# Weights of one attention and one scan layer split early, stored and reloaded; silu formed from tanh

## The chip, the cores and the metric

The kernel runs on one core of a Trainium2 chip. The metric is the device time of one execution in microseconds (us). The engines are TensorE (PE in the profile, with its weight loads as PEld), VectorE (DVE), ScalarE (ACT), GpSimd (POOL) and SyncE (SP), which here only issues DMAs.

## The reference

The reference sends 512 tokens of width 1024 through four layers, all in float32: a state-space mixer with a gated output (glu), an attention over a window of 128 tokens, a second state-space layer ("mamba"), and a full attention with two score maps. After the first and the second stands a feed-forward of width 4096 (`h + square(relu(hm @ w_up)) @ w_down`) and a gate (`h + sigmoid(norm(h) @ w_ple_gate) * (p @ w_ple_proj)`). What the change touches:

```python
k = (rmsnorm(h, kv_norm) @ w_k); v = (rmsnorm(h, kv_norm) @ w_v); q = rmsnorm(h, norm_mix) @ w_q
zxbcdt = rms_norm(x, norm_g) @ w_in                       # 1024 x 6176
z, xbc, dt_raw = zxbcdt[:2048], zxbcdt[2048:6144], zxbcdt[6144:]   # by columns
xbc = silu(causal_depthwise_conv(xbc, conv_w, conv_b))    # 4 taps
y = ssd_chunked_scan(xs * dt, a * dt, bm, cm) + d_skip * xs
u = y * silu(z); u = u * rsqrt(mean(u * u over 256 columns) + 1e-5) * gate_norm_g
```

## The kernel before, in words

Activations lie transposed: one tile holds 128 of the 1024 features by 512 tokens. To keep float32 accuracy on a faster matmul type (fp32r), every operand is split into two parts: `hi`, its rounding to fp32r, and `lo`, the rest. A product takes three matmuls (`three`): hi·hi, hi·lo and lo·hi.

Weights are split on the chip too. The class `Weights` holds the whole program's list of units (one DMA each, usually 1024 KB) and chunks (128 output columns by 1024 inputs, 24 matmuls each). `load_to` (L84) issues a unit's load on SP (L88) into one of three `raw` buffers. `split_to` (L92) multiplies a chunk by its norm gain on POOL where it has one (L100, 44 of the 289 chunks split on ACT: those of `w_k`, `w_v`, `w_q`, `w_kv_2` and `b_w_in_2`), rounds it on ACT (`whi`, L103) and subtracts on `lo_eng` (`wlo`, L104). `lo_eng` is DVE, but POOL during the q and v steps of the first attention and during mamba's input steps (L1139, L1410). `whi` and `wlo` have four buffers each. `take`, called by `gemm` before each chunk's matmuls, asks for the split of two chunks further on.

In the feed-forward (`mlp`, L890) the hidden 4096 columns go in two halves: `gemm` over 16 up chunks, whose `up` does relu and square on ACT, the square again on POOL and the rest on DVE; then 8 steps of two down chunks each, whose `down` adds to `h`. It has 64 chunks, and the kernel runs it twice.

In `mamba` (L1172) 48 chunks of `a_w_in_2` make z (16), B and C (8 each) and x (16). `conv` (L1263) takes a product through four taps and a `Silu` on ACT; `evac_z` takes z through `Silu`. Between these, the generator `ssd` does the scan of the previous group in small steps: per head it loads a row of the decay sums, broadcast to 128 partitions, from DRAM (`dec<-acs`, SP, L1331), forms `Exp` of it on ACT, multiplies on DVE, and PE takes the product (`yd`). `gate` (L1358) multiplies by silu(z), sums squares, and takes a root (`Sqrt`) in `rsqrt`. The ACT functions lie in tables that the compiler loads (`ACT_TABLE_LOAD`) when the function needed is not in the loaded one.

The order of instructions on each engine is not the order of the source: the program is built with `schedule_with_timeline_sim=True`, by which a planner reorders each engine's instructions by the times of its own model. Each engine, and SP's queue, then works in the fixed order it was given. Temporary tiles of 2 KB per partition come from 69 slots (`slot`, `drop`).

Of the kernel before, what the change touches and what calls it, by code (L numbers as in the profile page):

```python
# [11 lines left out]
F32 = mybir.dt.float32  # L12
F32R = mybir.dt.float32r
I32 = mybir.dt.int32
ACTF = mybir.ActivationFunctionType
# [47 lines left out]
class Weights:  # L63


    def __init__(self, nc, raw_pool, hl_pool, ahead_dma, ahead_split):
        self.nc, self.raw_pool, self.hl_pool = nc, raw_pool, hl_pool
        self.units, self.chunks = [], []
        self.loaded, self.split, self.used = 0, 0, 0
        self.ahead_dma, self.ahead_split = ahead_dma, ahead_split  # L70
        self.raw, self.hl = {}, {}
        self.lo_eng = nc.vector

    def add(self, w, k0, kt, c0, cols, cut=128, kg=8, gain=None):


        u = len(self.units)
        self.units.append((w[k0:k0 + 128 * kt, c0:c0 + cols].rearrange("(k p) n -> p k n", p=128), kt, cols))
        gain = None if gain is None else (gain, k0 // 128)
        new = [(u, k, min(kg, kt - k), c, min(cut, cols - c), gain) for c in range(0, cols, cut) for k in range(0, kt, kg)]  # L80
        self.chunks.extend(new)
        return new

    def load_to(self, u):  # L84
        while self.loaded < min(u, len(self.units)):
            ap, kt, cols = self.units[self.loaded]
            t = self.raw_pool.tile([128, kt, cols], F32, tag="raw", name="raw")
            self.nc.sync.dma_start(out=t, in_=ap)  # L88
            self.raw[self.loaded] = t
            self.loaded += 1  # L90

    def split_to(self, n):  # L92
        while self.split < min(n, len(self.chunks)):
            u, k, kn, c, cn, gain = self.chunks[self.split]
            self.load_to(u + self.ahead_dma)
            src = self.raw[u][:, k:k + kn, c:c + cn]
# [25 lines left out]
class Builder:  # L122
# [544 lines left out]
    def plan(self):  # L667
        W, ins = self.W, self.ins
        W.add(ins["w_ple_proj"][0], 0, 2, 0, D, cut=512)
        glu = ins["ssm_w_glu"][0]  # L670
        for m in range(0, 8, 2):
            n = len(W.chunks)
            a = W.add(glu, 0, 8, m * 128, 256)
            b = W.add(glu, 0, 8, D + m * 128, 256)
            W.chunks[n:] = [x for p in zip(a, b) for x in p]
        self.plan_mlp_gate(0)
        W.add(ins["w_k"], 0, 8, 0, 256, gain="kv")
        for m in range(0, 8, 2):
            if m == self.V_AT:
                W.add(ins["w_v"], 0, 8, 0, 256, cut=256, kg=4, gain="kv")  # L680
            W.add(ins["w_q"][0], 0, 8, m * 128, 256, gain="mix1")
        W.add(ins["w_ple_proj"][1], 0, 2, 0, D, cut=512)
        for m in range(0, 8, 2):
            W.add(ins["w_o"][0], 0, 8, m * 128, 256)
        self.plan_mlp_gate(1)
        w = ins["a_w_in_2"][0]
        W.add(w, 0, 8, 6144, 32)
        for g in range(self.Z_FIRST):
            W.add(w, 0, 8, 256 * g, 256)
        for g in range(8):  # L690
            W.add(w, 0, 8, 4096 + 128 * g, 128)
            W.add(w, 0, 8, 5120 + 128 * g, 128)
            W.add(w, 0, 8, 2048 + 256 * g, 256)
            if g in self.Z_AT:
                W.add(w, 0, 8, 256 * (self.Z_FIRST + self.Z_AT.index(g)), 256)
        for g in range(self.Z_FIRST + len(self.Z_AT), 8):
            W.add(w, 0, 8, 256 * g, 256)
        for m in range(8):
            W.add(ins["a_w_out_2"][0], 0, 16, m * 128, 128)
        for m in range(0, 8, 2):  # L700
            W.add(ins["w_kv_2"], 0, 8, m * 128, 256, gain="kv2")
        for c in range(2):
            for k0 in (0, 512):
                W.add(ins["w_kv_2"], k0, 4, D + c * 512, 512, cut=512, kg=2, gain="kv2")
        n, w = len(W.chunks), ins["b_w_in_2"][0]
        tiles = dict(x for m in range(0, 8, 2) for o in (0, 8)
                     for x in zip((o + m, o + m + 1), W.add(w, 0, 8, (o + m) * 128, 256, gain="b2")))
        W.chunks[n:] = [tiles[m] for m in self.QG]
        for k0 in (0, 512):
            W.add(ins["b_w_out_2"][0], k0, 4, 0, 512, cut=512, kg=2)  # L710
        for m in (4, 6):
            W.add(ins["b_w_out_2"][0], 0, 8, m * 128, 256, cut=256, kg=4)
# [9 lines left out]
            W.add(ins["w_ple_gate"][i], 0, 8, m * 128, 256)  # L722


    def gemm(self, n, xs, evac, lag=0, hook=None, hook_at=None):

        kt, pend, hook_at = len(xs), deque(), lag if hook_at is None else hook_at
        for m in range(n):
            ps = self.gbank()
            for k0 in range(0, kt, 8):  # L730
                whi, wlo = self.W.take()
# [158 lines left out]
    def mlp(self, xs, acc, name):  # L890
# [8 lines left out]
            r2.append(t)  # L899

        out, acc2 = [], self.slot(F32, "acc")
        for hf in range(2):
# [12 lines left out]
            def down(m, ps):  # L915
                t = self.slot(F32, "t")
                self.tt(t, ps, r2[0], MUL)
                self.tt(self.h[m], self.h[m], t, ADD)
                self.drop(t)
                if hf == 1:  # L920
                    self.square_in(acc2, self.h[m], m)
                    out.append(self.pair(self.h[m], self.g(name, m)))

            self.gemm(16, xs, up, 0 if hf else 1, None if hf else hook)
            if hf == 1:
                for p in xs:
                    self.drop(*p)
            self.gemm(8, hid, down)
            for p in hid:
                self.drop(*p)  # L930
        self.drop(r2[0])
        return out, acc2

    def side_input(self, i):
# [237 lines left out]
    def mamba(self, xs, acc1, acc2):  # L1172
# [8 lines left out]
        A.copy(out=cw, in_=ps[:, :160])  # L1181
        self.drop(*rows)

        hd = const.tile([128, 2, 32], F32, name="hd")
# [10 lines left out]
        with ExitStack() as cx:  # L1195
# [67 lines left out]
            def conv(t, ps):  # L1263
# [94 lines left out]
            def gate(g):  # L1358
# [9 lines left out]
                r = self.rsqrt(acc, 256.0, self.eps5)  # L1368
# [9 lines left out]
                ten[t] = conv((16 + g, 24 + g, 2 * g, 2 * g + 1)[i], ps)  # L1378

            def evac_z(t, ps):  # L1380
                x = self.slot(F32, "z")
# [265 lines left out]
def block_kernel(ctx: ExitStack, tc: tile.TileContext, ins, out, dbg=None):  # L1647
    nc = tc.nc
    b = Builder(ctx, tc, ins, out, dbg)
    raw = ctx.enter_context(tc.tile_pool(name="wraw", bufs=3))  # L1650
    hl = ctx.enter_context(tc.tile_pool(name="whl", bufs=4))
    b.W = Weights(nc, raw, hl, 2, 2)
    b.plan()
    b.add_slots(36, "f")

# [69 lines left out]
```

## Time and profile before

| | us |
|---|---|
| median of 3 runs (2044.8 to 2045.51) | 2044.87 |
| the profiled execution | 2044.02 |
| its span, first to last instruction | 2042.1 |
| PE busy | 1911.3 |
| DVE busy | 1182.1 |
| ACT busy | 970.2 |
| POOL busy | 582.2 |

The span in stages, by the trace: state-space mixer to 199, glu to 275, first feed-forward to 624, its gate and the first attention to 868, second feed-forward to 1197, its gate to about 1270, mamba to 1752 (of it the input steps and scan to 1664), second attention to the end. [...] A line like "PE a <- ACT b" in a list of waits says that PE stood still before it wrote a, until ACT had written b.

### The profile page before, as it was taken

The numbers are of one execution on the slowest core, as the hardware profiler recorded it, in microseconds if no ns is written. First come the engines' busy times: TensorE is split into PE (matmuls) and PEld (weight loads), VectorE is DVE, ScalarE is ACT, GpSimd is POOL, SyncE is SP. The second block draws the span as 40 slices with busy tenths as digits, with TensorE's granted clock in tenths as the row PEclk, the third lists the DMA queues.
The fourth block names the chain that finished last, engine by engine and source line by source line (L and its number), as shares of the span: only waits on it lengthen the run. The fifth ranks groups of instructions, "written<-read, shape, count | busy, mean of one in ns | idle before, by whom it ended". The sixth has DMA issues, their size and how long they took to land.

```text
span 2042.1 us, 25143 instructions
## 1 busy us (share of the span) xinstructions
PE 1911.3 (94%) x9486; PEld 1576.8 (77%) x9486; DVE 1182.1 (58%) x1912; ACT 970.2 (48%) x1734; POOL 582.2 (29%) x381
## 2 busy tenths in 40 slices
PE   2689999999999899999999999888899999999998
PEld 1678888888887787888888887667677788887888
DVE  7896553333447686543333456865457564727885
ACT  4554333223324377443233335587778843334553
POOL 6410122002116730221022008334444443432000
PEclk9899999999999899999999999999999999999999
DMA  4102333333332332232333321332233223335331
GB/s 118 26 6 87 115 104 90 96 103 96 90 103 93 93 115 65 83 104 83 103 104 91 95 86 51 97 104 75 73 101 124 86 74 117 116 91 138 110 94 42
DMA packets 232251, 185.82 MB, mean 91 GB/s; under 512 B 22803, under 2 KB 213982, under 8 KB 232130
## 3 DMA queue, kind: packets, MB, share of 16 engines
q1 hardware_dynamic: 219072, 179.43, 30.2%
q10 hardware_dynamic: 13058, 4.78, 1.0%
q8 instruction: 75, 1.23, 0.3%
q14 instruction: 46, 0.38, 0.1%
HBM read 166.03 MB, written 2.16 MB: 82 GB/s over the span
## 4 chain that ended last, share of the span: by engine, by line
PE 69%; DVE 13%; ACT 9%; issue 4%; POOL 2%; DMA 2%; SPq 0%; ACTq 0%; DVEq 0%; POOLq 0%
PE pg L192 63%; ACT L189 2%; ACT dec L189 2%; DVE lent L173 2%; PE pm L192 1%; PE sc L192 1%; ACT whi L103 1%; DVE dec L173 1%; DVE wlo L104 1%; DMA dec<-acs 1%; DVE pr L184 1%; ACT ea L189 1%; DVE cy L179 1%; DVE h L173 1%; PE po L192 1%
## 5 line engine op out<-in xcount | busy, mean ns | idle before, releaser
L103 ACT ACTIVATE whi<-raw 128x1024 fp32r<-128x1024 f32 x289 | 304.3, 1055 | 689.4 <-PE pg L192 594.9
L192 PE MATMUL pg<-xh,whi 128*128 128x512 f32 x1424 | 566.2, 398 | 10.4 <-ACT xh L189 5.0
L192 PE MATMUL pg<-xl,whi 128*128 128x512 f32 x1424 | 563.3, 396 | 7.4 <-DVE xl L173 7.4
L192 PE MATMUL pg<-xh,wlo 128*128 128x512 f32 x1424 | 561.2, 394 | 0.0
L104 DVE TENSOR_TENSOR wlo<-raw,whi 128x1024 fp32r<-128x1024 f32 (+1 forms) x229 | 296.5, 1297 | 369.1 <-ACT whi L103 369.0
L192 PEld LDWEIGHTS pg<-xh,whi 128*128 128x128 f32 x1424 | 270.5, 190 | 71.0 <-ACT xh L189 5.9
L192 PEld LDWEIGHTS pg<-xl,whi 128*128 128x128 f32 x1424 | 270.7, 190 | 68.3 <-DVE xl L173 10.0
L192 PEld LDWEIGHTS pg<-xh,wlo 128*128 128x128 f32 x1424 | 270.6, 190 | 56.9 <-issue 1.3
L176 POOL TENSOR_TENSOR b<-a 128x512 f32<-128x512 f32 x64 | 99.0, 1546 | 438.1 <-ACT a L189 418.6
L104 POOL TENSOR_TENSOR wlo<-raw,whi 128x1024 fp32r<-128x1024 f32 x60 | 145.3, 2425 | 211.2 <-ACT whi L103 201.3
L192 PE MATMUL pg<-hh,whi 128*128 128x512 f32 x512 | 199.2, 389 | 0.0
L192 PE MATMUL pg<-hl,whi 128*128 128x512 f32 x512 | 199.2, 389 | 0.0
L192 PE MATMUL pg<-hh,wlo 128*128 128x512 f32 x512 | 199.2, 389 | 0.0
L173 POOL TENSOR_TENSOR acc<-acc,sq 128x512 f32<-128x512 f32 x48 | 75.9, 1588 | 316.3 <-ACT sq L189 278.0
L100 POOL TENSOR_TENSOR raw<-raw,gv 128x1024 f32<-128x1024 f32 x44 | 94.5, 2168 | 138.9 <-DMA raw<-in_b_w_in_dram 81.0
L192 PEld LDWEIGHTS pg<-hh,whi 128*128 128x128 f32 x512 | 96.1, 188 | 20.1
L192 PEld LDWEIGHTS pg<-hh,wlo 128*128 128x128 f32 x512 | 96.1, 188 | 19.9
L192 PEld LDWEIGHTS pg<-hl,whi 128*128 128x128 f32 x512 | 96.1, 188 | 19.8
L189 ACT ACT_TABLE_LOAD x68 | 87.2, 1283 | 23.1 <-DVE cy L179 11.2
L173 DVE TENSOR_TENSOR t<-pg,r 128x512 f32<-128x512 f32 x48 | 32.7, 688 | 109.1 <-PE pg L192 109.0
L179 DVE SCALAR_TENSOR_TENSOR cy<-pg,cw,cy 128x511 f32<-128x511 f32 (+2 forms) x96 | 70.5, 738 | 43.4 <-ACT cy L189 42.8
L173 DVE TENSOR_TENSOR hl<-b,hh 128x512 fp32r<-128x512 f32 x64 | 44.1, 691 | 56.9 <-POOL b L176 56.9
(414 smaller groups left out, 3068.1 us busy)
## 6 DMA issues: line engine op xcount, KB each, us to landing
raw<-in_w_up_dram SPq DMA_DIRECT2D x32, 1024.0 KB
raw<-in_w_down_dram SPq DMA_DIRECT2D x32, 1024.0 KB
raw<-in_a_w_in_dram SPq DMA_DIRECT2D x16, 1024.0 KB
raw<-in_ssm_w_glu_dram SPq DMA_DIRECT2D x8, 1024.0 KB
raw<-in_w_ple_gate_dram SPq DMA_DIRECT2D x8, 1024.0 KB
raw<-in_a_w_in_dram SPq DMA_DIRECT2D x16, 512.0 KB
dec<-acs SPq DMA_DIRECT2D x32, 256.0 KB
raw<-in_a_w_out_dram SPq DMA_DIRECT2D x8, 1024.0 KB
```

Source lines behind the costliest of these rows:

```text
L100: self.nc.gpsimd.tensor_tensor(out=src, in0=src, in1=g, op=MUL)
L103: self.nc.scalar.activation(out=hi, in_=src, func=ACTF.Copy)
L104: self.lo_eng.tensor_tensor(out=lo, in0=src, in1=hi.bitcast(F32), op=SUB)
L173: (eng or self.V).tensor_tensor(out=out, in0=a, in1=b, op=op)
L176: self.G.tensor_tensor(out=out, in0=a, in1=b, op=op)
L179: self.V.scalar_tensor_tensor(out=out, in0=a, scalar=s, in1=b, op0=op0, op1=op1)
L184: eng.tensor_scalar(out=out, in0=a, scalar1=s1, scalar2=None, op0=op0)
L189: self.A.activation(out=out, in_=in_, func=func, **kw)
L192: self.T.matmul(out=out, lhsT=lhsT, rhs=rhs, start=start, stop=stop)
```

## The change

Sixty chunks (12 of the first attention: `w_k`, `w_v`, `w_q`; 48 of mamba's `a_w_in_2`) are marked `early`. They are no longer loaded and split beside their own matmuls. Instead each is cut in two pieces of 128 x 512, and `early_step` handles one piece in each of 60 calls per feed-forward: after each `up`, between the two chunks of a `down` step, and after it. A call stores the piece split in the call before (two DMAs of 256 KB, hi and lo, into a DRAM tile), loads a new piece (256 KB), and splits the piece loaded two calls before: gain on POOL if it has one, hi on ACT, lo on DVE. Each of these instructions is tied (`keep_in_program_order`) behind the one that stands before it in the source on its engine. Where the chunk is used, `split_to` only loads hi and lo from DRAM (512 KB each) into `whi` and `wlo`.

In mamba `Silu(y)` becomes `y' * (1 + Tanh(y'))` with `y' = y/2`: the taps and the bias are halved once, `Tanh` runs on ACT into a slot of its own and a `scalar_tensor_tensor` on DVE forms the product. For z it forms twice the silu; the norm's divisor (256 to 1024) and a halved gain take the factor out. The core of the diff:

```diff
+    def early_step(self, b, more=True):
+        nc, last = self.nc, b.tc.keep_in_program_order
+        if self.under_way and len(self.under_way[0]) == 3:
+            (chunk, h), raw, hi = self.under_way.popleft()
...
+            last(nc.sync.dma_start(out=self.kept[chunk][h, 0], in_=hi.bitcast(F32)))
+            last(nc.sync.dma_start(out=self.kept[chunk][h, 1], in_=raw))
+            b.drop(hi)
+        if more and self.n_early < len(self.early):
...
+            raw = self.early_pool.tile([128, 512], F32, tag="eraw", name="eraw", bufs=4)
+            last(nc.sync.dma_start(out=raw.rearrange("p (k n) -> p k n", k=n),
+                                   in_=self.units[u][0][:, k + h * n:k + h * n + n, c:c + cn]))
+            self.under_way.append(((chunk, h), raw))
...
+        if self.under_way and (len(self.under_way) > 2 or not more):
...
+                last(nc.gpsimd.tensor_tensor(out=x, in0=x, in1=g, op=MUL))
+            hi = b.slot(F32R, "ehi")
+            last(nc.scalar.activation(out=hi, in_=raw, func=ACTF.Copy))
+            last(nc.vector.tensor_tensor(out=raw.bitcast(F32R), in0=raw, in1=hi.bitcast(F32), op=SUB))
+            self.under_way[0] = (piece, raw, hi)
+    def early_end(self, b):
+        while self.under_way:
+            self.early_step(b, False)
...
     def split_to(self, n):
...
+            if self.units[u][3]:
+                hi = self.hl_pool.tile([128, kn, cn], F32R, tag="whi", name="whi")
+                lo = self.hl_pool.tile([128, kn, cn], F32R, tag="wlo", name="wlo")
+                for i, t in enumerate((hi, lo)):
...
+                    self.nc.sync.dma_start(out=t, in_=self.kept[chunk][:, i].rearrange("h p n -> p h n"))
...
@@ def up / def down / gemm(8, hid, down, between=half)
+                self.W.early_step(self)
...
+                if hf == 0 or m < 6:
+                    self.W.early_step(self)
+                elif m == 6:
+                    self.W.early_end(self)
@@ mamba: conv
-                self.act(y, y, ACTF.Silu)
+                u = self.slot(F32, "th")
+                self.act(u, y, ACTF.Tanh)
+                self.stt(y, u, 1.0, y, ADD, MUL)
+                self.drop(u)
@@ mamba: evac_z
-                    self.act(x, x, ACTF.Silu)
+                    self.act(u, x, ACTF.Tanh, scale=0.5)
+                    self.stt(x, u, 1.0, x, ADD, MUL)
...
-                    self.act(x, ps, ACTF.Silu)
+                    self.act(u, ps, ACTF.Tanh, scale=0.5)
+                    self.stt(x, u, 1.0, ps, ADD, MUL)
```

## Rows read from the trace of the kernel before

**Rows 1.** The page, parts 1 and 2: busy time by engine, granted clock.

```profile
PE 1911.3 (94%) x9486; PEld 1576.8 (77%) x9486; DVE 1182.1 (58%) x1912; ACT 970.2 (48%) x1734; POOL 582.2 (29%) x381
...
PEclk9899999999999899999999999999999999999999
```

**Rows 2.** Stretches: length, busy us of PE, PEld, DVE, ACT, POOL, PEclk, DMA share, GB/s.

```profile
275.40:624.30 348.90, 348.90 (x1541) 288.99 (x1540) 137.14 (x140) 115.41 (x147) 61.01 (x41) 1.00 0.33 98
624.30:690.00 65.70, 56.57 (x232) 43.93 (x232) 56.84 (x40) 30.20 (x42) 52.25 (x28) 0.94 0.21 66
690.00:818.00 128.00, 124.26 (x840) 104.36 (x840) 88.94 (x202) 83.72 (x235) 36.77 (x20) 0.99 0.36 99
1197.00:1270.00 73.00, 69.78 (x299) 54.72 (x298) 48.66 (x43) 33.55 (x49) 37.21 (x22) 0.98 0.21 61
1270.00:1317.00 47.00, 39.58 (x164) 31.00 (x163) 41.31 (x55) 27.38 (x34) 19.94 (x8) 0.93 0.31 90
1317.00:1664.50 347.50, 314.31 (x1652) 254.15 (x1651) 205.25 (x272) 257.39 (x414) 151.32 (x85) 0.97 0.31 92
```

**Rows 3.** Waits of PE, 1317 to 1664.5: total us, times, longest us.

```profile
PE xt L195 <- ACT r L189: 10.9, 3, 6.8
PE sum L192 <- DVE acc L173: 8.3, 3, 6.5
PE st L192 <- DVE xe L173: 3.7, 2, 3.2
```

**Rows 4.** Costliest groups, 1317 to 1664.5, columns as on the page's part 5.

```profile
L104 POOL TENSOR_TENSOR wlo<-raw,whi 128x1024 fp32r<-128x1024 f32 x39 | 94.5, 2422 | 169.6 <-ACT whi L103 159.8 <-PE xt L195 5.5 <-PE st L192 4.4
...
L189 ACT ACT_TABLE_LOAD x51 | 65.4, 1283 | 14.5 <-DVE cy L179 11.1 <-DMA dec<-acs 2.7
...
L103 ACT ACTIVATE whi<-raw 128x1024 fp32r<-128x1024 f32 x43 | 45.0, 1046 | 9.1 <-PE pg L192 6.5 <-issue 2.6
...
L173 DVE TENSOR_TENSOR dec<-dec,cb 128x512 f32<-128x512 f32 x32 | 39.5, 1263 | 11.7 <-ACT dec L189 11.4
...
L189 ACT ACTIVATE cy<-cy 128x512 f32<-128x512 f32 x30 | 18.9, 630 | 31.3 <-DVE cy L179 31.1
```

**Rows 5.** Chain that ended last, within 1400 to 1500: start us, us, what.

```profile
1440.90 4.09 DMA dec<-acs
...
1452.68 0.02 issue
1452.70 1.28 ACT L189
1453.99 0.01 issue
```

**Rows 6.** Costliest groups, 624 to 690.

```profile
L100 POOL TENSOR_TENSOR raw<-raw,gv 128x1024 f32<-128x1024 f32 x9 | 22.0, 2464 | 5.8 <-DMA raw<-in_w_q_dram 5.8
...
L173 DVE TENSOR_TENSOR xl<-h,xh 128x512 fp32r<-128x512 f32 x8 | 12.3, 1551 | 1.2 <-ACT xh L189 1.2
```

**Rows 7.** The tile tanh of the second attention: ns min/median/max, first and last start.

```profile
L189 ACT ACTIVATE tanh<-q x8: 620/642/651, 1854.1 to 1981.9; 128x512 f32<-128x512 f32 x8
L179 DVE SCALAR_TENSOR_TENSOR q<-tanh,q x8: 677/684/689, 1856.3 to 1984.1; 128x512 f32<-128x512 f32 x8
```

**Rows 8.** ACT's groups in the second attention, 1752 to 2042.

```profile
L189 ACT ACT_TABLE_LOAD x2 | 2.6, 1283 | 0.0
```

**Rows 9.** Costliest groups, first feed-forward, 275.4 to 624.3.

```profile
L173 DVE TENSOR_TENSOR hl<-b,hh 128x512 fp32r<-128x512 f32 x32 | 22.0, 691 | 28.0 <-POOL b L176 28.0
...
L189 ACT ACTIVATE hh<-a 128x512 fp32r<-128x512 f32 x32 | 20.2, 634 | 1.4
```

**Rows 10.** One 1024 KB weight load, by us, columns as in rows 2.

```profile
401.00:402.00 1.00, 1.00 (x7) 0.81 (x6) 0.00 (x0) 0.72 (x1) 0.00 (x0) 1.00 1.08 383
402.00:403.00 1.00, 1.00 (x6) 0.84 (x5) 0.63 (x1) 0.34 (x1) 0.00 (x0) 1.00 1.05 361
```

**Rows 11.** The output's stores to DRAM, same columns.

```profile
2038.00:2040.00 2.00, 0.00 (x0) 0.00 (x0) 0.34 (x1) 0.57 (x1) 0.00 (x0) 1.00 0.93 353
```

More of the change, by code (lines that the diff above doesn't have):

```diff
@@ L72, in __init__, with add @@
         self.lo_eng = nc.vector
-    def add(self, w, k0, kt, c0, cols, cut=128, kg=8, gain=None):
+        self.early, self.kept, self.n_early, self.under_way = [], {}, 0, deque()
+    def add(self, w, k0, kt, c0, cols, cut=128, kg=8, gain=None, early=False):
         u = len(self.units)
-        self.units.append((w[k0:k0 + 128 * kt, c0:c0 + cols].rearrange("(k p) n -> p k n", p=128), kt, cols))
+        self.units.append((w[k0:k0 + 128 * kt, c0:c0 + cols].rearrange("(k p) n -> p k n", p=128), kt, cols, early))
         gain = None if gain is None else (gain, k0 // 128)
@@ L81, in add @@
         self.chunks.extend(new)
-        return new
+        if early:
+            self.early.extend((x, h) for x in new for h in range(2))
+        return new
+    def early_step(self, b, more=True):
+        nc, last = self.nc, b.tc.keep_in_program_order
+        if self.under_way and len(self.under_way[0]) == 3:
+            (chunk, h), raw, hi = self.under_way.popleft()
+            if chunk not in self.kept:
+                self.kept[chunk] = self.dram.tile([2, 2, 128, 512], F32, name=f"kept{len(self.kept)}")
+            last(nc.sync.dma_start(out=self.kept[chunk][h, 0], in_=hi.bitcast(F32)))
+            last(nc.sync.dma_start(out=self.kept[chunk][h, 1], in_=raw))
+            b.drop(hi)
+        if more and self.n_early < len(self.early):
+            chunk, h = self.early[self.n_early]
+            self.n_early += 1
+            u, k, kn, c, cn, _ = chunk
+            n = kn // 2
+            raw = self.early_pool.tile([128, 512], F32, tag="eraw", name="eraw", bufs=4)
+            last(nc.sync.dma_start(out=raw.rearrange("p (k n) -> p k n", k=n),
+                                   in_=self.units[u][0][:, k + h * n:k + h * n + n, c:c + cn]))
+            self.under_way.append(((chunk, h), raw))
+        elif more:
+            more = False
+        if self.under_way and (len(self.under_way) > 2 or not more):
+            piece, raw = self.under_way[0]
+            (u, k, kn, c, cn, gain), h = piece
+            if gain is not None:
+                n = kn // 2
+                o = self.gcol[gain[0]] + gain[1] + k + h * n
+                g = self.gains[:, o:o + n].unsqueeze(2).to_broadcast([128, n, cn])
+                x = raw.rearrange("p (k n) -> p k n", k=n)
+                last(nc.gpsimd.tensor_tensor(out=x, in0=x, in1=g, op=MUL))
[3 more added lines that the diff above has]
+            self.under_way[0] = (piece, raw, hi)
@@ L84, in load_to @@
+    def early_end(self, b):
+        while self.under_way:
+            self.early_step(b, False)
     def load_to(self, u):
         while self.loaded < min(u, len(self.units)):
-            ap, kt, cols = self.units[self.loaded]
+            ap, kt, cols, early = self.units[self.loaded]
+            if early:
+                self.loaded += 1
+                continue
             t = self.raw_pool.tile([128, kt, cols], F32, tag="raw", name="raw")
@@ L93, in split_to @@
         while self.split < min(n, len(self.chunks)):
-            u, k, kn, c, cn, gain = self.chunks[self.split]
+            u, k, kn, c, cn, gain = chunk = self.chunks[self.split]
             self.load_to(u + self.ahead_dma)
+            if self.units[u][3]:
+                hi = self.hl_pool.tile([128, kn, cn], F32R, tag="whi", name="whi")
+                lo = self.hl_pool.tile([128, kn, cn], F32R, tag="wlo", name="wlo")
+                for i, t in enumerate((hi, lo)):
+                    t = t.rearrange("p k n -> p (k n)").bitcast(F32).rearrange("p (h n) -> p h n", h=2)
+                    self.nc.sync.dma_start(out=t, in_=self.kept[chunk][:, i].rearrange("h p n -> p h n"))
+                self.hl[self.split] = (hi, lo)
+                self.split += 1
+                continue
             src = self.raw[u][:, k:k + kn, c:c + cn]
@@ L676, in plan @@
         self.plan_mlp_gate(0)
-        W.add(ins["w_k"], 0, 8, 0, 256, gain="kv")
+        W.add(ins["w_k"], 0, 8, 0, 256, gain="kv", early=True)
         for m in range(0, 8, 2):
             if m == self.V_AT:
-                W.add(ins["w_v"], 0, 8, 0, 256, cut=256, kg=4, gain="kv")
-            W.add(ins["w_q"][0], 0, 8, m * 128, 256, gain="mix1")
+                W.add(ins["w_v"], 0, 8, 0, 256, cut=256, kg=4, gain="kv", early=True)
+            W.add(ins["w_q"][0], 0, 8, m * 128, 256, gain="mix1", early=True)
         W.add(ins["w_ple_proj"][1], 0, 2, 0, D, cut=512)
@@ L688, in plan @@
         for g in range(self.Z_FIRST):
-            W.add(w, 0, 8, 256 * g, 256)
+            W.add(w, 0, 8, 256 * g, 256, early=True)
         for g in range(8):
-            W.add(w, 0, 8, 4096 + 128 * g, 128)
-            W.add(w, 0, 8, 5120 + 128 * g, 128)
-            W.add(w, 0, 8, 2048 + 256 * g, 256)
+            W.add(w, 0, 8, 4096 + 128 * g, 128, early=True)
+            W.add(w, 0, 8, 5120 + 128 * g, 128, early=True)
+            W.add(w, 0, 8, 2048 + 256 * g, 256, early=True)
             if g in self.Z_AT:
-                W.add(w, 0, 8, 256 * (self.Z_FIRST + self.Z_AT.index(g)), 256)
+                W.add(w, 0, 8, 256 * (self.Z_FIRST + self.Z_AT.index(g)), 256, early=True)
         for g in range(self.Z_FIRST + len(self.Z_AT), 8):
-            W.add(w, 0, 8, 256 * g, 256)
+            W.add(w, 0, 8, 256 * g, 256, early=True)
         for m in range(8):
@@ L722, in plan_mlp_gate, with gemm @@
             W.add(ins["w_ple_gate"][i], 0, 8, m * 128, 256)
-    def gemm(self, n, xs, evac, lag=0, hook=None, hook_at=None):
+    def gemm(self, n, xs, evac, lag=0, hook=None, hook_at=None, between=None):
         kt, pend, hook_at = len(xs), deque(), lag if hook_at is None else hook_at
@@ L730, in gemm @@
             for k0 in range(0, kt, 8):
+                if k0 and between:
+                    between(m)
                 whi, wlo = self.W.take()
@@ L901, in mlp @@
         out, acc2 = [], self.slot(F32, "acc")
+        cx = ExitStack()
+        self.W.early_pool = cx.enter_context(self.tc.tile_pool(name="early" + name, bufs=1))
         for hf in range(2):
@@ L927, in mlp, with half @@
                     self.drop(*p)
-            self.gemm(8, hid, down)
+            def half(m):
+                if hf == 0 or m < 6:
+                    self.W.early_step(self)
+            self.gemm(8, hid, down, between=half)
             for p in hid:
@@ L931, in mlp @@
         self.drop(r2[0])
+        cx.close()
         return out, acc2
@@ L1180, in mamba @@
         self.tr(ps[:, 128:160], rows[1][0:32, 0:128], 32)
-        A.copy(out=cw, in_=ps[:, :160])
+        self.act(cw, ps[:, :160], ACTF.Copy, scale=0.5)
+        g2 = self.gv[:, self.gcol["gate2"]:self.gcol["gate2"] + 16]
+        self.ts(g2, g2, 0.5, MUL)
         self.drop(*rows)
@@ L1367, in gate @@
                     self.square_in(acc, xT[p], p, last=1)
-                r = self.rsqrt(acc, 256.0, self.eps5)
+                r = self.rsqrt(acc, 1024.0, self.eps5)
                 for p in range(2):
@@ L1380, in evac_z @@
             def evac_z(t, ps):
-                x = self.slot(F32, "z")
+                x, u = self.slot(F32, "z"), self.slot(F32, "th")
                 if t < 2 * self.Z_FIRST:
                     self.tt(x, ps, rr[0], MUL)
-                    self.act(x, x, ACTF.Silu)
+                    self.act(u, x, ACTF.Tanh, scale=0.5)
+                    self.stt(x, u, 1.0, x, ADD, MUL)
                     for m in range(2 * t, 2 * t + 2):
@@ L1387, in evac_z @@
                 else:
-                    self.act(x, ps, ACTF.Silu)
+                    self.act(u, ps, ACTF.Tanh, scale=0.5)
+                    self.stt(x, u, 1.0, ps, ADD, MUL)
+                self.drop(u)
                 zs[t] = x
@@ L1652, in block_kernel @@
     b.W = Weights(nc, raw, hl, 2, 2)
+    b.W.dram = ctx.enter_context(tc.tile_pool(name="wkept", bufs=1, space=bass.MemoryType.DRAM))
     b.plan()
```

## The prediction

> **What bounds the kernel now.** I read the page first: PE is busy for 1911.3 us of a span of 2042.1 [rows 1], so 130.8 us are left in which it stands still, and the granted clock falls below full speed in only a few slices. Next I cut the span into stages [rows 2]. In the first feed-forward PE is busy in all of its 348.9 us at full clock; with 64 chunks of 24 matmuls that is 5.45 us a chunk. Nothing done there beside PE can be gained back there, and work added there is free as long as the splits keep ahead. PE stands still where the changed weights are used: 65.70 - 56.57 = 9.1 us around the first gate, 3.7 us in the first attention, 3.2 us and 7.4 us on the way into mamba, and 33.2 us in the scan stretch, 1317 to 1664.5. The lower clock adds to it: in the scan stretch, 314.31 x (1 - 0.97) = 9.4 us of PE's busy time would not be there at full clock, and around the first gate 56.57 x 0.06 = 3.4 us.
>
> Third, the waits of PE in the scan stretch [rows 3]. The two largest, 10.9 and 8.3 us, end with ACT (the second by way of a DVE add that itself waits for ACT's square). ACT is busy for 257.39 of 347.5 us there, 74%, more than any engine but PE [rows 2]. What fills it is in the groups [rows 4]: 51 table loads take 65.4 us and 43 weight roundings 45.0 us, together 110 of the 257. POOL's subtractions take 94.5 us and slow DVE: a `dec` product takes 1263 ns there, where a product of the same shape in the feed-forward takes 691 [rows 4, 9]. So the scan is PE's work, with gaps that a crowded ACT makes.
>
> **The change, part by part.** The sum is made against the profiled execution, 2044.02 us (span 2042.1 and 1.9 around it); the median of the runs shown is 0.85 higher.
>
> *Feed-forward steps, added: no cost.* Each of the two has 60 calls. One call adds a rounding of 128x512 on ACT, taken as 634 ns from the square of that shape and type, and a subtraction on DVE of 691 ns [rows 9]. ACT rises from 115.4 by 38.0 to 153.4 us of 348.9, DVE from 137.1 by 41.5 to 178.6 [rows 2]. The 24 attention pieces add a gain product on POOL each, half of 2464 ns [rows 6], 29.6 us on 61.0. All three stay near or below half. What hides them is PE's queue: splits are asked for two chunks, 10.9 us, ahead, and one call delays the next split by about 0.6 us on ACT and 0.7 on DVE. If that cover were gone, each call would cost its 1.3 us on PE, 159 us in all, the far end.
>
> SP's queue gets three DMAs a call, each tied behind the weight load before it in the source; a store waits for hi and lo that were asked for one call, 5.45 us, earlier, so it should not hold the next weight load. The bytes: 98 GB/s now, at a DMA share of 0.33, hence 297 GB/s at full share [rows 2]; 786 KB more in 5.45 us are 144 GB/s, together 242. A burst of one load ran at 383 and 361 GB/s [rows 10], and the output's stores at 353 GB/s at a share of 0.93 [rows 11], so a byte stored costs what a byte loaded costs. I take zero. If stores cost double, the share would be 0.33 x (1 + 0.5 + 2) = 1.16 and each call would last 0.16 x 5.45 = 0.87 us longer, 105 us over 120 calls.
>
> *Around the first gate (624 to 690): 6 us gained.* POOL is busy for 52.25 of 65.7 us, of which the gain products are 22.0 [rows 2, 6]; those of `w_k`, `w_v` and `w_q` leave. DVE's `xl`, on the way to the next matmul, takes 1551 ns beside POOL [rows 6] against 691 for a subtraction of that shape [rows 9]: 8 x 0.86 = 6.9 us of DVE. What stays late is the chain after the last gate tile and the root before `k`. I take half of the 9.1 us idle and half of the 3.4 us of clock. Ends: 0 and 12.5.
>
> *First attention (690 to 818): 1.5 us gained* of 3.7 idle and 1.2 clock. Here a pair of 512 KB loads can stand before the many small SP transfers; one 1024 KB at 372 GB/s takes 2.8 us [rows 10]. Ends: 4.9 gained; lost, one such delay for each of the 10 rotations, 28 us, if none were covered.
>
> *Into mamba (1197 to 1317): 0.5 us gained.* DVE is busy in 41.31 of the 47 us after 1270 [rows 2]. Four z tiles add a product of 684 ns [rows 7], 2.7 us, while POOL's subtractions, which slow DVE, go. Ends: 3 lost, 5 gained.
>
> *Scan stretch: 27.5 us gained.* Removed on ACT: 43 roundings, 45.0 us. Tanh costs 642 ns and Silu 630 [rows 4, 7], so that swap is free on ACT itself. Table loads: in the second attention Exp and Tanh alternate through 290 us with 2 loads [rows 8], so they share a table; what is left to switch for is the root in `gate`, two loads for each of eight groups, 16. 35 of 51 loads go, 44.9 us. ACT falls to 257.4 - 45.0 - 44.9 = 167.5, 48% of the stretch. On DVE 42 products are added (30 `conv`, 12 z) at 684 ns [rows 7], 28.7 us; against it 32 `dec` products get 572 ns shorter, 18.3 us: 205.3 becomes 215.7, 62%. POOL falls to 56.8. All are well below PE, whose work at full clock is 314.31 x 0.97 = 304.9. Of the 33.2 us idle, 19.2 hang on ACT [rows 3]; I let a quarter of them stay, 4.8. Of the other 14.0 I let half stay, 7.0, since DVE's own lateness came in part from ACT and POOL. That leaves 11.8; 21.4 go. The clock's 9.4 shrink with the idle time to 3.3; 6.1 go. What is late next is DVE, with the root's reciprocal and the new product between ACT and PE. Ends: 0, and all 42.6; a loss is the third rival's.
>
> The loads of hi and lo themselves: 2.8 us a pair [rows 10], asked for when the buffer's former chunk is done, three chunks (16 us) before use. No cost; with the cover gone, 2.8 us for each of 48 chunks, 134 us.
>
> [...]
>
> Sum: 6 + 1.5 + 0.5 + 27.5 = 35.5. 2044.02 - 35.5 = 2008.5, and 0.85 more for the median: 2009.
>
> **The rivals.**
>
> *PE reaches its floor.* All idle time and clock loss of the scan (42.6) and three quarters of the gate's (9.4) go: 52 us, 1993. For it: ACT and POOL lose most of what crowds them. Against: 14 of the 33 us are not waits for ACT.
>
> *The waits move to DVE.* `conv` now ends ACT, DVE, PE where it ended ACT, PE, and the planner's order may put the product late. Then only a few gaps close: 10 us gained, 2034. Against: DVE would be busy for 62%, and its largest part gets shorter.
>
> *The decay rows come late: slower.* `dec<-acs` stands in the chain with 4.09 us [rows 5] and is queued on SP among the loads, which double in bytes. A row behind a pair lands 2.8 us later [rows 10], and its chain of ACT and DVE no longer hides behind a crowded ACT. There are 32 rows. It decides from 13 of them fully exposed (35.5 / 2.8); at 24 it would be 67 us against 35.5, 2076. Against: DMA share is 0.31 there [rows 2].
>
> *Feed-forward bound by DMA: slower.* The 105 us above: 2114. Against: the stores' price [rows 11].
>
> *Tables are still switched.* If Tanh were served from another table than Exp, 45 us of ACT would stay and I would expect half of the scan's gain: 2023. Against: [rows 8].
>
> **How the numbers follow.** Forecast 0.58, floor 0.13, DVE 0.15, decay rows 0.06, DMA 0.02, tables 0.06. The forecast's own range is 1998 to 2022. The range 1991 to 2034 takes in the floor and the DVE case and leaves out the two slower ones. About 0.2% is what can be told from no change; faster has all but the slower cases and a fifth of the DVE case: 0.89, same 0.03, slower 0.08.
>
> **What would show it.** Right: in the feed-forward PE busy throughout, still 349 us, with a DMA share near 0.8; in mamba about 20 table loads, no `whi` on ACT, DVE's `dec` near 700 ns, PE's idle time near 12 us in the scan, clock 0.99. Wrong: PE waiting in the feed-forward for `whi` or `wlo`; PE waiting in the scan for `whi<-kept` DMAs or `dec`; a scan stretch as long as before with ACT idle.

## The result, and the profile after

The changed kernel takes 1992.63 us (median of 4 runs) against 2045.19 us: a ratio of 0.9745, 95% interval 0.9728 to 0.9762, or 52.6 us less. The forecast was 2009, the range 1991 to 2034: the time lies in the range, but outside the forecast's own 1998 to 2022; it is the number of the first rival (PE reaches its floor, 1993). The profiled execution took 1990.7 us with a span of 1988.9.

Page, parts 1 and 2, of the changed kernel; it answers to [rows 1]:

```profile
PE 1898.5 (95%) x9486; PEld 1571.7 (79%) x9486; DVE 1234.8 (62%) x2075; ACT 927.0 (47%) x1752; POOL 446.5 (22%) x339
...
PEclk9799999999999999999999999999999999999999
...
DMA packets 322277, 311.76 MB, mean 157 GB/s; under 512 B 29875, under 2 KB 242558, under 8 KB 322146
```

PE's busy time fell by 13 us although it issues the same 9486 matmuls; most of this is the scan, where 337.78 us at a granted clock of 0.96 of full speed became 325.90 us at 1.00 (lines below); POOL lost 136 us; the DMAs move 312 MB where they moved 186. The stages of the changed kernel, columns as in [rows 2]; the bounds of the second, third and last are moved to events that both kernels have (the first product of `col`, the last product with v, the end of the dt products, the first matmul of the scan):

```profile
275.20:624.10 348.90, 348.90 (x1541) 288.90 (x1540) 187.43 (x201) 149.95 (x207) 85.14 (x63) 1.00 0.75 233
624.10:680.00 55.90, 53.61 (x225) 42.57 (x223) 35.88 (x33) 23.41 (x35) 21.66 (x16) 0.97 0.40 143
680.00:816.80 136.80, 127.35 (x847) 108.17 (x847) 81.01 (x205) 78.99 (x230) 18.92 (x13) 0.96 0.39 113
1196.00:1263.00 67.00, 65.62 (x287) 51.41 (x286) 45.28 (x43) 33.00 (x49) 33.07 (x21) 1.00 0.41 129
1263.00:1285.30 22.30, 18.71 (x80) 14.05 (x78) 16.20 (x19) 11.50 (x17) 0.00 (x0) 1.00 0.66 236
1285.30:1611.20 325.90, 325.90 (x1749) 267.13 (x1750) 234.47 (x357) 176.45 (x344) 62.49 (x48) 1.00 0.49 162
```

And the kernel before, cut at the same events:

```profile
624.30:686.70 62.40, 55.10 (x224) 42.54 (x223) 53.64 (x36) 29.15 (x41) 48.95 (x26) 0.95 0.21 68
686.70:817.60 130.90, 125.33 (x847) 105.52 (x847) 92.14 (x206) 84.71 (x236) 40.06 (x22) 0.99 0.35 98
1197.00:1269.60 72.60, 69.38 (x298) 54.45 (x297) 48.66 (x43) 33.55 (x49) 37.21 (x22) 0.98 0.21 61
1269.60:1293.50 23.90, 16.51 (x69) 11.97 (x67) 18.34 (x17) 17.41 (x22) 12.73 (x5) 0.93 0.31 88
1293.50:1664.50 371.00, 337.78 (x1747) 273.45 (x1748) 228.23 (x309) 267.36 (x426) 158.53 (x88) 0.96 0.31 92
```

| stage | before | after | won | forecast |
|---|---|---|---|---|
| first feed-forward | 348.9 | 348.9 | 0 | 0 |
| around the first gate | 62.4 | 55.9 | 6.5 | 6 |
| first attention | 130.9 | 136.8 | -5.9 | 1.5 |
| second gate, dt | 72.6 | 67.0 | 5.6 | with the next: 0.5 |
| to the scan | 23.9 | 22.3 | 1.6 | |
| scan | 371.0 | 325.9 | 45.1 | 27.5 |

These sum to 52.9; the spans differ by 53.2. The scan begins here 23.5 us earlier than the stretch that the forecast called the scan, so the last three rows are best read together: 52.3 us won, 28.0 forecast. In the feed-forward PE does not stand still once though the DMA share rose from 0.33 to 0.75; the second feed-forward took 328.4 us before and takes 328.3. In the scan PE is busy in all of 325.9 us at full clock; before, 337.78 us at 0.96 would be, by my estimate (337.78 x 0.96), 324 us at full clock, so the scan is at PE's floor. None of the waits of [rows 3] is left. The groups of the scan that answer to [rows 4], same columns:

```profile
L235 DVE SCALAR_TENSOR_TENSOR cy<-th,cy 128x512 f32<-128x512 f32 x32 | 22.7, 709 | 6.7 <-ACT th L245 6.7
...
L229 DVE TENSOR_TENSOR dec<-dec,cb 128x512 f32<-128x512 f32 x32 | 20.9, 685 | 6.9 <-ACT dec L245 6.7
...
L245 ACT ACT_TABLE_LOAD x11 | 14.1, 1283 | 3.5 <-DVE cy L235 3.3
...
L160 POOL TENSOR_TENSOR wlo<-raw,whi 128x1024 fp32r<-128x1024 f32 x2 | 4.8, 2393 | 7.4 <-DMA lamw<-in_b_lambda_dram 6.6 <-ACT whi L159 0.8
```

The same stretch of the kernel before has 53 table loads and 42 of POOL's subtractions (51 and 39 in the shorter one of [rows 4]); now there are 11 and 2, and DVE's `dec` products take 685 ns instead of 1263. In the attention PE has new waits (total us, times, longest):

```profile
PE pg L248 <- DMA whi<-kept: 3.4, 1, 3.4
PE pm L251 <- DMA pn<-in_p_dram: 3.1, 1, 3.1
```

The reload it waits for was issued late. SP's queue around it (start us, length, instruction); between 693.99 and 698.20 only small transfers stand, left out here:

```profile
681.66 0.39 SPq L148 DMA_DIRECT2D wlo<-kept  x1
...
693.99 0.59 SPq L1115 DMA_DIRECT2D kl<-lo  x1
...
698.20 0.39 SPq L148 DMA_DIRECT2D whi<-kept  x1
```

SP did not stand still here: 24 issues (16 copies of k, 8 small transfers) of 0.53 to 0.72 us each lie between the first and the last of these lines.

### The profile page after: what moved, and what is told of

It reads as the page before. It is cut to its first block, busy times and chain, and to the rows that moved or that the text cites. A ratio compares the mean times of both kernels' runs of the same rounds, so it can differ in the third digit from the quotient of the medians.

```text
span 1988.9 us, 26217 instructions
## 1 busy us (share of the span) xinstructions
PE 1898.5 (95%) x9486; PEld 1571.7 (79%) x9486; DVE 1234.8 (62%) x2075; ACT 927.0 (47%) x1752; POOL 446.5 (22%) x339
## 5 line engine op out<-in xcount | busy, mean ns | idle before, releaser
L248 PE MATMUL pg<-xh,whi 128*128 128x512 f32 x1424 | 560.1, 395 | 6.4 <-DMA whi<-kept 3.4
L159 ACT ACTIVATE whi<-raw 128x1024 fp32r<-128x1024 f32 (+1 forms) x229 | 241.4, 1056 | 473.2 <-PE pg L248 422.5
L160 DVE TENSOR_TENSOR wlo<-raw,whi 128x1024 fp32r<-128x1024 f32 (+1 forms) x223 | 283.7, 1275 | 278.7 <-ACT whi L159 271.9
L119 ACT ACTIVATE ehi<-eraw 128x512 fp32r<-128x512 f32 x120 | 74.7, 624 | 105.0 <-DMA eraw<-in_a_w_in_dram 56.2
L120 DVE TENSOR_TENSOR eraw<-eraw,ehi 128x512 fp32r<-128x512 f32 x120 | 83.4, 696 | 50.3 <-ACT ehi L119 48.2
L156 POOL TENSOR_TENSOR raw<-raw,gv 128x1024 f32<-128x1024 f32 x32 | 64.5, 2036 | 127.3 <-DMA raw<-in_b_w_in_dram 57.6
L229 DVE TENSOR_TENSOR hl<-b,hh 128x512 fp32r<-128x512 f32 x64 | 55.6, 871 | 56.9 <-POOL b L232 55.9
```

What stands on the lines that cost most here:

```text
L119: last(nc.scalar.activation(out=hi, in_=raw, func=ACTF.Copy))
L120: last(nc.vector.tensor_tensor(out=raw.bitcast(F32R), in0=raw, in1=hi.bitcast(F32), op=SUB))
L229: (eng or self.V).tensor_tensor(out=out, in0=a, in1=b, op=op)
L248: self.T.matmul(out=out, lhsT=lhsT, rhs=rhs, start=start, stop=stop)
```

## The experiments

The first four take the change apart. Ratios are to the kernel before in runs on the same chip.

**Tanh without early splits**

```diff
-        W.add(..., early=True)
+        W.add(..., early=False)   # all twelve places
```

> Only the silu from tanh; no chunk is split early. In the changed kernel the scan stretch (about 371 us before, 326 after) has 11 table loads where there were 51, 51 us less on ACT, while this kernel keeps the 45 us of roundings on ACT and the 95 us of subtractions on POOL. Theory 1, ACT's crowding as a whole held PE and both halves count alike: half of the scan's 45 us, about 2022 us. Theory 2, the table loads alone decide, because they sit in the chain between two ACT steps: 40 us or more in the scan, about 2005 us. Theory 3, POOL's subtractions beside DVE decide: within 5 us of before, about 2041 us.

Measured 2020.96 us, ratio 0.9872 (0.9856 to 0.9889): 26.8 us won. From its last dt product to its last `sum` 456.1 us pass (before 481.7, changed kernel 434.4). The scan, and three groups from 1270 to 1645, a little more than the scan (in the scan alone 43 subtractions, 104.5 us, and 11 table loads):

```profile
1292.70:1641.00 348.30, 332.58 (x1749) 270.35 (x1750) 279.89 (x359) 212.63 (x386) 161.59 (x89) 0.98 0.34 98
```

```profile
L160 POOL TENSOR_TENSOR wlo<-raw,whi 128x1024 fp32r<-128x1024 f32 x47 | 114.6, 2441 | 146.2 <-ACT whi L159 135.1 <-PE st L248 4.8 <-PE cb L248 3.9
...
L229 DVE TENSOR_TENSOR dec<-dec,cb 128x512 f32<-128x512 f32 x32 | 29.1, 919 | 11.0 <-ACT dec L245 10.8
...
L245 ACT ACT_TABLE_LOAD x15 | 19.2, 1283 | 2.8 <-DVE cy L235 2.6
```

ACT is down to 213 of 348 us, yet PE still stands still for 15.7 us, and its longest waits (6.0, 5.4 and 3.4 us) end with DVE. DVE is now busy for 280 us: it makes the new products, and with POOL's subtractions beside it its `dec` products take 919 ns. Theory 1 by its number; it turned out that this does not name the engine.

**Early splits with Silu**

```diff
-                self.act(u, y, ACTF.Tanh)
-                self.stt(y, u, 1.0, y, ADD, MUL)
+                self.act(y, y, ACTF.Silu)   # and so for z, divisor and gains as before
```

> Only the early splits; Silu is kept, so some 50 table loads stay in mamba. Outside the scan it should gain the 6 us around the first gate, lose the 6 us in the first attention, and gain some 5 us before mamba, as the changed kernel does. Theory 1: half of the scan's gain, about 2017 us. Theory 2 (table loads decide): within 6 us in the scan, about 2035 us. Theory 3 (POOL's subtractions decide): most of the 45 us, about 1997 us.

Measured 1998.90 us, ratio 0.9764 (0.9749 to 0.9779): 48.9 us won, nearly all. Its scan, and its table loads from 1260 to 1625 (50 of the 54, 64.2 us, lie in the scan):

```profile
1282.30:1617.00 334.70, 327.29 (x1747) 267.72 (x1747) 204.93 (x309) 226.22 (x384) 62.35 (x48) 0.99 0.49 159
```

```profile
L245 ACT ACT_TABLE_LOAD x54 | 69.3, 1283 | 27.5 <-DVE cy L235 18.5 <-DVE z L229 4.8 <-DMA dec<-acs 3.3
```

With 50 table loads in the scan PE stands still for 7 us only. Theory 3's number came closest (1997), theories 1 and 2 fall: the early splits alone bring most. Once these are there, the table loads are worth about 4 us of the whole, with intervals that overlap the changed kernel's, and 6 to 9 us of mamba's length (443.3 us; see the table below).

**Only mamba's chunks early**

```diff
-        W.add(ins["w_k"], 0, 8, 0, 256, gain="kv", early=True)
+        W.add(ins["w_k"], 0, 8, 0, 256, gain="kv", early=False)   # and so w_v, w_q
```

> As the changed kernel, but the 12 chunks of w_k, w_v and w_q are loaded and split beside their matmuls as before; only mamba's 48 chunks are split early. Theory: in the changed kernel the 6.5 us won around the first gate are given back in the attention, so this kernel has the first gate at 62 us and the attention at 131 us again, and the same time as the changed kernel within 2 us (1991 to 1995 us). Rival: the attention's loss is an accident of the planner's order and has nothing to do with the reloads; then the attention stays near 137 us and the time is 6 us worse, about 1999 us.

Measured 1993.97 us, ratio 0.9743 (0.9729 to 0.9758), the changed kernel's own. Gate and attention, here cut at the copy of `col`:

```profile
625.00:688.10 63.10, 55.24 (x231) 42.97 (x230) 55.85 (x38) 30.21 (x42) 53.77 (x29) 0.97 0.22 69
688.10:814.50 126.40, 122.59 (x838) 103.48 (x839) 89.98 (x204) 83.58 (x234) 37.83 (x20) 1.00 0.37 101
```

The gate is back at 63.1 us, the attention even at 126.4 (before, at this cut, 128.2; changed kernel 135.3). The theory holds: what the twelve chunks win around the gate they give back. Gate and attention together take 189.5 us here, 192.7 in the changed kernel and 193.3 before, so they give back even more than they win; the whole is not faster for it, as mamba takes 437.7 us here against 434.4.

**The attention's reloads from POOL**

```diff
+                q = self.nc.gpsimd if gain is not None else self.nc.sync
-                    self.nc.sync.dma_start(out=t, in_=self.kept[chunk]...)
+                    q.dma_start(out=t, in_=self.kept[chunk]...)
```

> As the changed kernel, but the reloads of the attention's 12 chunks are issued from POOL instead of SP. In the changed kernel PE waits 4 us in the attention for a reloaded chunk, whose load was issued on SP 16 us after the one before it, behind the copies of k and the small transfers of q. Theory 1, SP's fixed order delays the reload: the wait goes and the attention falls from 136.8 to about 131 us, 1987 us in all. Theory 2, the 1024 KB a chunk are too many for the DMA engines there (share 0.98 from 700 to 720 us): the wait stays wherever the load is issued, within 2 us of 1993 us.

Measured 1989.07 us, ratio 0.9714 (0.9700 to 0.9729). Gate and attention at the same cut as above:

```profile
624.40:678.60 54.20, 52.86 (x233) 42.87 (x232) 37.38 (x36) 23.30 (x35) 33.05 (x30) 1.00 0.46 156
678.60:811.60 133.00, 125.52 (x839) 105.37 (x837) 80.52 (x203) 78.72 (x229) 25.89 (x23) 0.97 0.40 113
```

PE's waits from 624 to 812:

```profile
PE sc L249 <- ACT pr L246: 3.8, 2, 3.0
PE pT L252 <- DVE pr L241: 1.8, 1, 1.8
PE pg L249 <- DVE rx L230: 1.1, 1, 1.1
PE pm L252 <- DMA pn<-in_p_dram: 1.0, 1, 1.0
```

No wait for a reload is left, so theory 1 is right on that wait; but the attention shortened by 2.3 us, not 6, and PE now waits for ACT's `pr` and others. The gate shortened too, from 57.4 us at this cut to 54.2, so the two together gained 5.5. This kernel has the lowest time of all that were measured. Against the changed kernel (0.9736, interval 0.9722 to 0.9751, in the yardstick run below) the intervals overlap, so that it beats it is likely and not shown.

The next six put one load back into mamba, or double one. One length can be read in every run's profiled execution: from the start of the last dt product to that of the last `sum`, which is nearly all of mamba.

| kernel | us |
|---|---|
| before | 481.7 |
| Tanh without early splits | 456.1 |
| early splits with Silu | 443.3 |
| changed kernel (twice), and the three that change only the attention's chunks | 434.4 to 437.7 |
| a rounding back on ACT | 438.9 |
| a subtraction back on POOL | 470.3 |
| the same with 8 columns | 436.0 |
| the new product twice | 437.2 |
| a third load per chunk | 454.0 |
| the third load from DRAM to DRAM | 437.1 |

The fourth row is the same mamba in five runs; its spread of 3.3 us is what can't be told from no change.

**A rounding back on ACT**

```diff
+                if gain is None and self.junk_pool is not None:      # inside mamba
+                    junk = self.junk_pool.tile([128, kn, cn], F32R, tag="junk", name="junk", bufs=1)
+                    self.nc.scalar.activation(out=junk, in_=hi.bitcast(F32), func=ACTF.Copy)
```

> The changed kernel with one rounding of 128x1024 put back on ACT for each chunk reloaded inside mamba (its result goes unused), some 45 of 1050 ns, 47 us; POOL stays free and Tanh stays. Early splitting alone brought 38 us in mamba and Tanh alone 26 us, so each by itself removes most of the gaps. Theory 1, ACT's load as a whole decides: ACT goes from 176 to about 223 us in the scan's 326, and part of the gaps come back, as many as in the kernel with early splits and Silu (58 us of table loads more on ACT), which needed 9 us longer: about 8 us more than the changed kernel, 2001 us. Theory 2, what counts is POOL and the DVE that it slows: within 2 us of the changed kernel, 1993 us.

Measured 1997.32 us, ratio 0.9763 (0.9748 to 0.9777): some 4 us more than the changed kernel, but the intervals overlap (0.9728 to 0.9762). ACT rose to 213 of 326 us and PE stands still for 1.4:

```profile
1286.00:1612.00 326.00, 324.61 (x1739) 266.47 (x1739) 233.08 (x354) 212.98 (x383) 61.63 (x48) 0.99 0.49 162
```

The time lies midway between the theories (2001 and 1993) and decides for neither. What it does show: 43 us of roundings back on ACT cost mamba 1 to 4.5 us, so ACT's crowding is worth little once POOL is free.

**A subtraction back on POOL**

```diff
-                    self.nc.scalar.activation(out=junk, in_=hi.bitcast(F32), func=ACTF.Copy)
+                    self.nc.gpsimd.tensor_tensor(out=junk, in0=hi.bitcast(F32), in1=lo.bitcast(F32), op=SUB)
```

> The changed kernel with one subtraction of 128x1024 put back on POOL for each chunk reloaded inside mamba (its result goes unused), some 45 of 2.4 us, 108 us; ACT stays free. Theory 1, ACT decides: within 3 us of the changed kernel, 1993 to 1996 us, though DVE's dec products go back from 685 towards 1263 ns. Theory 2, POOL and the DVE that it slows decide: most of the 22 us that lie in mamba between Tanh alone and the changed kernel come back, about 2010 us.

Measured 2033.46 us, ratio 0.9943 (0.9928 to 0.9958): 41 us lost, more than theory 2 said. Groups of its scan:

```profile
L152 POOL TENSOR_TENSOR junk<-whi,wlo 128x1024 fp32r<-128x1024 f32 x42 | 103.9, 2473 | 147.0 <-DMA wlo<-kept 146.9
...
L233 DVE TENSOR_TENSOR dec<-dec,cb 128x512 f32<-128x512 f32 x32 | 37.5, 1195 | 7.9 <-ACT dec L249 7.9
```

```profile
1290.00:1650.00 360.00, 335.89 (x1747) 273.05 (x1748) 282.85 (x359) 175.06 (x344) 162.54 (x89) 0.96 0.44 147
```

PE's waits from 1285 to 1650:

```profile
PE yo L252 <- DVE st L233: 5.4, 5, 1.8
...
PE yo L252 <- DVE st L1400: 4.0, 4, 1.3
PE yd L252 <- DVE dec L233: 4.0, 1, 4.0
```

DVE's `dec` are back at 1195 ns, and DVE was busy for 283 of 360 us. All of PE's waits in that list but 1.9 us end with DVE, and none with a reload, so it is not that POOL holds the buffers of hi and lo longer. PE stands still for 24 us, and at a clock of 0.96 it is busy for 10 us more than in the changed kernel's scan. The 41 us are not the price of the old subtractions, though: with Tanh alone POOL makes 104.5 us of them in the scan, with ACT's roundings beside them, and mamba takes 456.1 us, here 470.3. POOL also waited 147 us for the loads, in its fixed order, so this run mixed two things. The next one parts them.

**The same with 8 columns**

```diff
-  self.nc.gpsimd.tensor_tensor(out=junk, in0=hi.bitcast(F32), in1=lo.bitcast(F32), op=SUB)
+  self.nc.gpsimd.tensor_tensor(out=junk[:, 0, 0:8], in0=hi.bitcast(F32)[:, 0, 0:8], in1=lo.bitcast(F32)[:, 0, 0:8], op=SUB)
```

> As the kernel with the subtraction put back on POOL (2033 us), but the subtraction takes 128x8 elements only: POOL still waits in its fixed order for each reloaded chunk (147 us of waiting there), and is busy for some 0.1 us each instead of 2.47. Theory 1, what costs is POOL's busy time, by its own lateness and by slowing DVE (the dec products went from 685 to 1195 ns): the 40 us go, 1993 to 1998 us. Theory 2, the waiting costs, because POOL's products for the scan stand behind it: most of the 40 us stay, 2020 us or more.

Measured 1993.41 us, ratio 0.9742 (0.9727 to 0.9756): the 40 us are gone. Groups of the scan:

```profile
L233 DVE TENSOR_TENSOR dec<-dec,cb 128x512 f32<-128x512 f32 x32 | 20.9, 684 | 6.2 <-ACT dec L249 6.1
...
L152 POOL TENSOR_TENSOR junk<-whi,wlo 128x8 fp32r<-128x8 f32 x41 | 15.1, 369 | 199.0 <-DMA wlo<-kept 199.0
```

POOL waits longer than before, 199 us, and it costs nothing; a subtraction of 128x8 takes 369 ns, not 0.1 us, and the `dec` are at 684 ns. Theory 1: POOL's busy time is what costs. It can do so by slowing DVE and by making POOL's own later products late; which of these two paths carries how much was not separated.

**The new product twice**

```diff
+                u2 = self.slot(F32, "th2")
+                self.stt(u2, u, 1.0, y, ADD, MUL)
                 self.stt(y, u, 1.0, y, ADD, MUL)    # and so in evac_z from PSUM
```

> The changed kernel with each new DVE product of conv and of most z tiles done twice, 44 more of about 0.7 us, 31 us on DVE in the scan, which goes from 234 to 265 of 326 us. It tests the rival that DVE is late next. Theory 1, PE is at its floor in the scan and DVE has room: within 3 us of the changed kernel, 1993 to 1996 us. Rival: DVE, with the product between ACT and PE, sets the scan's end already; then at least half of the 31 us show, 2008 us or more.

Measured 1994.52 us, ratio 0.9748 (0.9734 to 0.9763): no difference. DVE as the next bound falls.

**A third load per chunk**

```diff
+                    self.nc.sync.dma_start(out=t, in_=self.kept[chunk][:, 0].rearrange("h p n -> p h n"))   # t: a view of junk
```

> The changed kernel with a third load of 512 KB for each chunk reloaded inside mamba (into a buffer that nothing reads), 24 MB more, DMA share in the scan from 0.49 to about 0.7. It tests the rival that decay rows come late behind the reloads. Theory 1, the rows have slack: within 2 us of the changed kernel, 1993 to 1995 us. Rival: each of 32 rows is 1.4 us later and reaches PE; then 20 to 45 us more, 2013 us or above.

Measured 2011.94 us, ratio 0.9829 (0.9813 to 0.9846): 19 us lost. PE's two largest waits from 1285 to 1632, and SP's second largest:

```profile
PE pg L254 <- DVE xl L235: 3.6, 1, 3.6
PE pg L254 <- DMA whi<-kept: 3.6, 1, 3.6
```

```profile
SPq L154 <- DMA junk<-kept: 89.5, 28, 5.2
```

The time is close to the rival's number, but its cause is not seen: ACT's waits for decay rows sum to 25.2 us here and to 21.0 in the changed kernel. SP stood 90 us waiting for the one spare buffer, with decay rows and reloads behind it. Its largest wait, for a free `whi` buffer, is 103.9 us here and 179.2 in the changed kernel, and all its waits together are 278 us here and 273 there, so SP does not stand longer in sum. The run does not say whether the bytes or the order of SP's waits cost the 19 us.

**The third load from DRAM to DRAM**

```diff
+                    spare = self.dram.tile([2, 128, 512], F32, name=f"spare{self.split}")
+                    self.nc.sync.dma_start(out=spare, in_=self.kept[chunk][:, 0])
```

> As the kernel with a third load for each chunk (2012 us), but the 512 KB are copied from DRAM to DRAM, each to a place of its own, so that SP waits for no buffer. In the kernel before, SP stood 90 us waiting for its one spare buffer, with decay rows and reloads behind. Theory 1, that standing still cost the 19 us, not the bytes: within 3 us of the changed kernel, 1993 to 1996 us. Theory 2, the bytes make rows or reloads late: 10 us or more, 2003 us or above.

Measured 2320.65 us, ratio 1.1341 (1.1322 to 1.1360). It answers another question: needing no buffer in mamba, the copies were moved by the planner into the feed-forward, right behind the stores they read. Mamba itself took 437.1 us between the events above (434.4 in the changed kernel). SP's queue and the DMA in the second feed-forward:

```profile
1502.62 0.59 SPq L152 DMA_DIRECT2D spare<-kept  x1
1503.31 0.39 SPq L105 DMA_DIRECT2D eraw<-in_a_w_in_dram  x1
1503.80 0.45 SPq L136 DMA_DIRECT2D raw<-in_w_ple_gate_dram  x1
1504.31 8.88 SPq L96 DMA_DIRECT2D kept<-ehi  x1
```

```profile
1508.00:1511.00 3.00, 3.00 (x15) 2.49 (x14) 0.00 (x0) 0.00 (x0) 0.00 (x0) 1.00 0.28 98
1511.00:1514.00 3.00, 3.00 (x15) 2.49 (x14) 0.00 (x0) 0.00 (x0) 0.00 (x0) 1.00 0.19 78
...
1517.00:1520.00 3.00, 0.00 (x0) 0.00 (x0) 2.66 (x4) 1.92 (x3) 0.00 (x0) 0.86 0.13 48
```

After a copy the DMA share fell to 0.19 and 0.13, and the store that is issued third behind it held SP for 8.9 us. ACT's tied roundings waited 378.8 us for their pieces from 275 to 1580 us, and PE stood still behind ACT (for `hh` 67.7 us). Why the share falls is not shown, nor which transfers ran in these windows. Whether more bytes alone delay the scan stays open.

**Six of the attention's chunks early, and a yardstick**

```diff
-            W.add(ins["w_q"][0], 0, 8, m * 128, 256, gain="mix1", early=True)
+            W.add(ins["w_q"][0], 0, 8, m * 128, 256, gain="mix1", early=m < self.V_AT)   # and reloads from POOL
```

> As the kernel with the attention's reloads on POOL's queue, but only six of the attention's chunks are early (w_k, the first two of w_q, w_v); the last six of w_q are loaded and split beside their matmuls. The first gate should keep its 54 us and the attention (to the last product with v) should come down from 133 towards the 126 us of the kernel that splits none of its chunks early. Theory: 1984 us, 5 us faster than with all twelve. Rival: the attention's 126 us come from its late start, since work that used to lie before it must then lie in it; then no faster than with all twelve, 1989 us.

> The changed kernel unchanged, as a yardstick on the same chip for the three others: 0.9745 of the kernel before.

Measured 1997.63 us, ratio 0.9761 (0.9747 to 0.9776), and for the yardstick 1992.15, 0.9736 (0.9722 to 0.9751). The theory falls, and the rival is right only in that it is not faster: it is slower than with all twelve, with intervals that do not overlap. The loss is in the gate and not in the attention: cut at the copy of `col`, the gate takes 61.0 us (54.2 with all twelve) and the attention 132.1 (133.0). POOL is busy for 42.5 us in that gate up to 680 alone, 33.1 with all twelve. That the gain products of the last six chunks, back on POOL, are the cause is not shown.

## Why the prediction was right, and where it was off

*The mechanism* held: work taken from the stretches with gaps into the feed-forward, where PE is busy throughout, is paid nowhere. The step "Feed-forward steps, added: no cost" is exact (348.9 and 348.9 us; DMA share 0.75 for "near 0.8").

The range holds the time because it took in the floor's number; the forecast's own case, gaps that stay in part, did not come.

*The scan term was mis-sized*: 27.5 forecast, 45.1 measured (with *Into mamba*, 28.0 and 52.3). Of the 33.2 us idle I let 11.8 stay, and 3.3 of the clock's 9.4; nothing stayed. I named ACT because PE's longest waits ended with it [rows 3]. The runs put POOL first: of the 47.3 us by which mamba got shorter (481.7 to 434.4), early splits alone take 38.4 and Tanh alone 25.6. Once both are in place, a subtraction put back on POOL costs 41 us of the whole, a rounding put back on ACT about 4 and the table loads about 4; in the whole time neither of these two is clear of the noise. Naming ACT was not wrong, since easing it alone won more than half; wrong was the size of what POOL does, which I had entered only as 18.3 us of DVE time. How ACT came to stand last in the list is a reading and not shown by a run of its own: in [rows 4] ACT waited 31.1 us for DVE's `cy` before `Silu`, so ACT was late behind DVE work, of which POOL slowed `dec` (1263 ns against 685) but not the conv's own steps for `cy` (738 ns before, 741 after). The single shares do not add up, since either relief closes gaps that the other would close too, and PE's floor caps the sum; and the POOL run, whose subtraction waits for a reload, is not quite the old one.

*Into mamba*, 0.5 forecast, 7.2 measured up to the scan as cut here, was mis-sized in the same way. The dt products take 18.6 us from first to last start in the kernel with Tanh alone, 18.5 before, and 12.8 or 12.9 in the kernels with mamba's chunks early, but 17.4 where a subtraction is put back on POOL and 14.8 with the third load.

*First attention*, 1.5 forecast, 5.9 lost. The step priced a delay behind reloads for the small transfers; what came was the reverse, a reload queued behind the copies of k on SP. That wait is 4 us and goes when another queue issues the reload. The rest is in part PE's clock, from which the step expected a gain of up to 1.2 us: with all twelve chunks reloaded from POOL the attention takes 133.0 us, of which PE is busy for 125.52 at a clock of 0.97, with none early 126.4, of which 122.59 at 1.00. So 2.9 of these 6.6 us are busy time and 3.7 are waits, the largest for the softmax on ACT and DVE. Why PE waits more there is not shown; that it arrives earlier, with the softmax as late as before, would fit.

*Rivals.* The floor was right in kind and number (1993). DVE as next bound is refuted by the doubled product. Tables switched on: 11 loads left, refuted. Decay rows late: ACT does wait longer for them, 21.0 us in the scan against 6.5 before, but none of it reaches PE; how near they are, the third-load runs leave open. DMA-bound feed-forward: refuted at 233 GB/s.

That POOL's subtractions slow DVE's `dec` is measured: `dec` takes 1263 ns with them, 919 with them beside Tanh, 685 without, 1195 with them put back, 684 with 8 columns. By what means is not shown.

## What to carry to other kernels

Where one stage has an engine to spare and a later one does not, work on constants can be done early and parked in DRAM; check that stage's slack engine by engine, and the queue that the reload stands in where it is used. A wait list names who came last, not who made it late: before sizing a gain, look for the engine whose removal shortens instructions elsewhere, and put each removed load back alone to find it.

## What the runs showed that was not expected

POOL waiting 199 us in its order for loads cost nothing (1993.41 us against 1992.63), while 104 us of POOL subtractions behind the same loads cost 40 us of the whole. SP waits 273 us in the changed kernel's scan, 179 of them for a free buffer, at no cost to PE. Behind a DRAM to DRAM copy of 512 KB the DMA share fell to 0.19 and 0.13, and a store's issue on the same queue took 8.9 us. A pair of 512 KB loads issued from POOL landed 5.2 and 5.4 us after issue (median), and the DMAs carried 233 GB/s of loads and stores through a whole feed-forward beside a PE that was busy in all of its 348.9 us at a clock of 1.00.
